# Position bias of a hybrid decoder step: tables laid out on the host in place of tables built on the chip and spread in DRAM

## The chip, the cores and the metric

The kernel runs on one core of one Trainium2 chip. The metric is the device time of one execution in microseconds; the runs of the kernel before have a median of 2324.24 us. The engines are TensorE (PE for its matmuls, PEld for its weight loads), VectorE (DVE), ScalarE (ACT), GpSimd (POOL) and SyncE (SP). Transfers run on 16 DMA engines. SP's transfers travel on queue q1 ("hardware dynamic" in the profile), POOL's on queue q0 ("software dynamic").

## What is computed

One step of a two-layer decoder on 320 tokens, 256 of a prompt and 64 of eight sample sequences of eight tokens. A layer projects x (2048 channels) to 13824 columns, runs three branches on them and merges these:

```python
h = x @ w_in
oa, s_new = retention(qa, ka, va, s_ret, pos0)
p = multi_scale_pool(u_ext, pos0, T)
oc = window_attention(qc, k_ext, v_ext, pos0, sinks, rel_bias)
merged = sigmoid(ma) * ya + sigmoid(mb) * yb + sigmoid(mc) * yc
x_new = layer_norm(alpha * x + merged @ w_out, ln_g, ln_b)
```

The change touches the window attention. It has 16 heads in 4 key groups, a window of 128 and a bias on the scores that depends on head and distance alone (32 buckets of distances; beyond the window a score is masked):

```python
dist = arange(bq)[:, None] + WINDOW - arange(span)[None, :]
bias = rel_bias[t5_bucket(maximum(dist, 0))]
s = where(valid, s + bias, finfo(float32).min)
```

The sample sequences also attend to 128 cached keys and values each (`cache_win_k`, `cache_win_v`).

## The kernel before, in words

All weights are cut on the host into 128 x 128 blocks in the order of use, eight blocks to a chunk of 512 KB. `load` (line 148) fetches a chunk from SP's queue, `split_h` (ACT, the copy of line 177) and `split_l` (mostly DVE, line 184) split it into a high and a low part, and a block takes three matmuls of 128 x 128 by 320 columns (line 198). A chunk is 24 such matmuls. In `run`, while TensorE works on chunk c, ACT and DVE split chunk c + 2, and SP is given the load of chunk c + 6. Four tiles `w` hold raw chunks, three `h` and three `l` hold split ones, so a load waits until the split of an older chunk has freed a tile.

After each chunk `pump` lets background work emit a step: `setup`, the attention, the retention and the pooling are generators. This fixes each engine's own order of instructions, but not the time: an engine runs ahead until it meets a wait. `setup` gives POOL almost nothing but transfers.

The order at the start: SP loads x and the first chunks in turns; x is split too (`xh` by ACT, `xl` by DVE). The first product group takes eight chunks, along with x as it comes.

The bias before: `setup` loads the 32 buckets of 16 heads to `rb` (line 323), memsets `zt` [16, 384], fills it by one ACT copy and 16 small DVE copies (line 331), then POOL writes `zt` 128 times into a DRAM tile `zd` [16, 128, 384] (line 336, 3 MB). Behind it on POOL stand the loads of the constants: `dmask`, `qdec`, `maskS`, `kdec`, `kdecS`, `cnt`, `pscale`, `lng`, `lnb`, `bmask`, `flip` (line 138). Reading `zd` with a row step of 383 gives each query's row a shift by one. So `load_bias` in `attention` (line 825) reads [128, 4, 256] in rows of 1 KB on SP, twice for each of two head pairs and layers, and the table of the samples, `biasS` [128, 4, 160], is memset and filled by 32 small transfers on SP (line 361). The cached values `cv` come from a natural layout in rows of 512 B (`done_kc`, line 763), the cached keys `ck` by partition.

Of the kernel before, what the change touches and what calls it, by code (L numbers as in the profile page):

```python
# [11 lines left out]
F32 = mybir.dt.float32  # L12
# [6 lines left out]
DEPTH = 2  # L19
NP = 256                 # prompt tokens, columns 0..255  # L20
NB, NT = 8, 8            # sample sequences and their tokens, columns 256 + 8 b + t
# [3 lines left out]
POOL_BUF = 15  # L25
POOL_W = (2, 4, 8, 16)
EXT = POOL_BUF + NP      # prompt part of a pooling row, then NB parts of HW
# [4 lines left out]
ROW = 128 * 384  # L32
# [6 lines left out]
CH = 8                   # weight blocks of 128 x 128 in a chunk  # L39


def att_rows(t):
    """Columns of tile t = 4 P + g of the attention: head (2P, g), then head (2P + 1, g)."""
    p, g = divmod(t, 4)
    lo, hi = (2 * p) * 4 + g, (2 * p + 1) * 4 + g
    return np.concatenate([np.arange(lo * 64, lo * 64 + 64), np.arange(hi * 64, hi * 64 + 64)])
# [6 lines left out]
def layer_groups():  # L53
    """Products of a layer in their order; the jobs of one group share their K loop."""
    g = [[("kc", 0), ("vc", 0), ("qc", 0), ("qc", 1)]]
    g += [[("qc", t)] for t in (2, 3)]
    g += [[("kc", 1)], [("vc", 1)]] + [[("qc", t)] for t in (4, 5, 6, 7)]
    late = [("ub", i) for i in range(8)]
    for h in range(HA):
        late += [("qa", h), ("ka", h), ("va", 2 * h), ("va", 2 * h + 1)]  # L60
    for i, job in enumerate(late):
        g.append([job])
        if i in (4, 6, 8, 10):
            g += [[("pm", i - 4)], [("pm", i - 3)]]
    for b in "bac":
        g += [[("g" + b, i)] for i in range(8)]
        for j in range(0, 16, 2):
            g += [[("m" + b, j)], [("m" + b, j + 1)], [("y" + b, j)], [("y" + b, j + 1)]]
    g += [[("wo", j)] for j in range(16)]
    return g  # L70


def layer_blocks():
    """(kind, index, k) of each 128 x 128 block of weights, in the order of use."""
    out = []
    for grp in layer_groups():
        for k in range(n_k(grp[0][0])):
            out += [(kind, i, k) for kind, i in grp]
    return out
# [7 lines left out]
def free(ap):  # L87
    """Elements of a partition."""
    return math.prod(ap.shape[1:])
# [9 lines left out]
class Step:  # L99
    def __init__(self, ctx, tc, io):  # L100
        self.tc, self.nc, self.io = tc, tc.nc, io
        pool = lambda n, b, **kw: ctx.enter_context(tc.tile_pool(name=n, bufs=b, **kw))
        self.cp = pool("const", 1)
        self.gp = pool("gran", 24)
        self.mp = pool("mid", 13)
        self.np = pool("mini", 6)
        self.sp = pool("small", 8)
        self.wp = pool("w", 4)
        self.hp = pool("wh", 3)
        self.lp = pool("wl", 3)  # L110
        self.pd = pool("psd", 3, space=bass.MemoryType.PSUM)
        self.pp = pool("psp", 5, space=bass.MemoryType.PSUM)
        self.dp = pool("dram", 1, space=bass.MemoryType.DRAM)
        self.raw, self.H, self.L = {}, {}, {}
        self.busy = {"a": 0.0, "v": 0.0, "p": 0.0}
        self.lanes = {"att": deque(), "ret0": deque(), "ret1": deque()}
        self.misc = []

# [81 lines left out]
    def add_mm(self, out, lhsT, rhs):  # L200
        """Adds to a part of what an earlier matmul of the bank wrote."""
        self.nc.tensor.matmul(out, lhsT=lhsT, rhs=rhs, start=False, stop=True, skip_group_check=True)  # L202
# [6 lines left out]
    def hl(self, h, lo, src):  # L209
        """The two parts of src whose sum it is."""  # L210
        self.copy(h, src)
        self.tt(lo, src, h.bitcast(F32), ALU.subtract)

    def rsqrt(self, y, v, t):
        """y = v ** -0.5 of t = v ** 0.5, with one step of Newton's."""
        self.busy["v"] += 0.8
        self.nc.vector.reciprocal(out=y, in_=t)
        self.stt(t, y, -0.5, y, ALU.mult, ALU.mult)
        self.tt(t, t, v, ALU.mult)
        self.stt(y, t, 1.5, y, ALU.add, ALU.mult)  # L220

    def sums(self, out, src, first):
        """Sums over the partitions, of the tokens 80 g + i at partitions 32 g.. and column i."""
        for g in range(4):
            o = out[32 * g:32 * g + 32, :]
            a = src[:, 80 * g:80 * g + 80]
            if first:
                self.mm(o, self.ones[:, 0:32], a)
            else:
                self.add_mm(o, self.ones[:, 0:32], a)  # L230

    def fold(self, y):
        """For spread(): of a group's 32 equal rows one with the high part of y, the next the low one."""
# [8 lines left out]
    def spread(self, r):  # L242
        """The inverse of the order of sums(): a row of all tokens at each partition."""
        ps = self.p([128, T])
        self.mm(ps, self.ones_r, r.rearrange("p g i -> p (g i)"))
        return ps

    def token_sums(self, src):
        """Sums over the partitions, with tokens 0.., 128.. and 192.. at the partitions of a column."""
# [5 lines left out]
    def token_rows(self, y):  # L255
        """The inverse of token_sums() for y: a row of all tokens at each partition."""
# [26 lines left out]
    def pump(self):  # L283
        """Once a chunk: background steps, as far as the other engines keep up with TensorE."""
# [16 lines left out]
    def setup(self):  # L301
# [19 lines left out]
        zt = self.m([16, 384], name="zt")  # L321
        rb = self.m([16, 32], name="rb")
        nc.sync.dma_start(out=rb, in_=io["rel"])
        nc.vector.memset(zt, NEG)
        yield
        yield
        self.copy(zt[:, 240:256], rb[:, 16:32])
        for n in range(16, 32):
            a = BUCKET_START[n]
            b = (BUCKET_START + [128])[n + 1] - 1  # L330
            nc.vector.tensor_copy(
                out=zt[:, 255 - b:256 - a],
                in_=rb[:, 31 - n:32 - n].to_broadcast([16, b - a + 1]),
            )
        zd = self.dp.tile([16, 128, 384], F32, name="zd")
        nc.gpsimd.dma_start(out=zd, in_=zt.unsqueeze(1).to_broadcast([16, 128, 384]))
        self.zd = zd[:]
        yield
# [12 lines left out]
        self.biasS = self.const("biasS", [128, 4, 160])  # L351
        nc.vector.memset(self.biasS, NEG)
        for _ in range(8):
            yield
        for kv in range(4):
            row = self.zd.offset + 4 * kv * ROW
            for b4 in range(4):
                r = slice(32 * b4, 32 * b4 + 32)
                for o, n, c0 in ((127, 128, 0), (255, 8, 128 + 8 * b4)):
                    src = bass.AP(self.zd.tensor, row + o, [[ROW, 4], [383, 8], [1, n]])  # L360
                    nc.sync.dma_start(out=self.biasS[r, kv, c0:c0 + n], in_=src)
                if b4 % 2:
                    yield

# [72 lines left out]
    def block_low(self, jobs, k):  # L437
        """The products with the low parts of the activations; the end of the jobs."""
# [55 lines left out]
    def before(self, kind, i):  # L494
# [4 lines left out]
        if kind == "mb" and i == 0:  # L499
            for o, src in (("o_wkc", "ckr"), ("o_wvc", "cv")):  # L500
# [254 lines left out]
    def done_kc(self, p, ps):  # L755
# [7 lines left out]
        nc.sync.dma_start(  # L763
            out=cv, in_=self.io["cv"][l, :, :, 128 * p:128 * p + 128].rearrange("b s d -> s b d")
        )
# [15 lines left out]
    def softmax(self, s, n, sink, nsink):  # L781
        """s: n score tiles [128, keys] in a row, normalised in place, in three stages."""
# [22 lines left out]
    def attention(self, l, p, a):  # L805
# [15 lines left out]
        def load_bias(hf):  # L821
            b = self.g([128, 4, 256], name="bias")
            row = 4 * (2 * p + hf) * ROW
            src = bass.AP(self.zd.tensor, self.zd.offset + row + 127, [[383, 128], [ROW, 4], [1, 256]])
            nc.sync.dma_start(out=b, in_=src)
# [19 lines left out]
        # second block's scores: rows of q's two parts against k's high part, then q's high part and k's low one  # L845
# [15 lines left out]
        def soft(make, out):  # L861
            """The stages of one softmax: scores, softmax (3), what comes of it."""
# [12 lines left out]
        def block0(hf):  # L875
            """The first 128 queries: their own keys."""
# [27 lines left out]
        def block1(hf, g):  # L904
            """The other queries: all keys of both blocks."""
# [34 lines left out]
        def sample(c):  # L940
            """Four sequences: rows 32 b + 8 g + t, the cached keys and the new ones of the four."""
# [268 lines left out]

def weight_blocks(a):
# [89 lines left out]
```

## Time and profile before

| | |
|---|---|
| median of 3 runs | 2324.24 us (2323.37 to 2325.18) |
| profiled execution, span | 2325.7 us |
| PE busy | 2275.5 us (98%) |
| DVE, ACT, POOL busy | 1221.6, 946.1, 183.8 us |
| chain that ended last | PE 91%, DVE 5%, DMA 2%, ACT 1% |
| DMA, mean over the span | 154 GB/s |

How to read it: the page cuts the span into 40 slices of 58 us and gives each engine's busy share in tenths, then the clock that TensorE was granted, then the DMA engines' busy share. The groups name line, engine, operation and tiles as out<-in. The lists of waits name who waited for whom. A timeline row has start, duration, engine, line, operation, tiles, shape and count, and in brackets the idle time of that engine just before and what ended it. A row of a stretch table has the stretch, its length, then busy time and instruction count of PE, PEld, DVE, ACT and POOL, then the granted clock as a share of 2.4 GHz, the DMA engines' busy share and GB/s.

### The profile page before, as it was taken

To read this page: it belongs to the slowest core of one execution; us is meant where nothing else is said; L and a number is where in the kernel's file an instruction comes from. 1 tells how busy PE (TensorE), PEld (TensorE's weight loads), DVE (VectorE), ACT (ScalarE), POOL (GpSimd) and SP (SyncE) were. 2 spreads that over 40 slices of the span, in tenths; PEclk is the share of its full clock that TensorE was granted. 3 is DMA by queue.
4 is the path that set the end of the run, shared out by engine and by line. 5 is a ranking of instruction groups with operands and counts; after the bars stand their busy time and mean duration, and the time that the engine had idled before them with its cause. 6 is when DMAs were issued, how large, how long until landed. Compare 5 with 4: busy or idle time off the path is not lost.

```text
span 2325.7 us, 37758 instructions
## 1 busy us (share of the span) xinstructions
PE 2275.5 (98%) x15660; PEld 2219.8 (95%) x15660; DVE 1221.6 (53%) x1844; ACT 946.1 (41%) x1537; POOL 183.8 (8%) x190
## 2 busy tenths in 40 slices
PE   8799999999999999999999999999999999999997
PEld 8697999999999999999998989999999999999997
DVE  4459555443444444446666785554344444444566
ACT  4354444433333334333355444453334333433333
POOL 0114100000000000000041140000000000000001
PEclk9899999999999999999999999999999999999998
DMA  8743545444444444444444334544444444444442
GB/s 224 215 140 107 171 154 198 167 145 154 145 154 145 154 147 153 145 155 145 150 162 138 138 128 157 192 175 154 153 146 146 153 154 145 146 154 147 153 146 99
DMA packets 106091, 358.00 MB, mean 154 GB/s; under 512 B 12192, under 2 KB 21344, under 8 KB 105856
## 3 DMA queue, kind: packets, MB, share of 16 engines
q1 hardware_dynamic: 101152, 336.15, 42.1%
q0 software_dynamic: 4768, 19.45, 3.1%
q8 instruction: 122, 2.00, 0.3%
q14 instruction: 49, 0.40, 0.1%
HBM read 338.46 MB, written 21.03 MB: 155 GB/s over the span
## 4 chain that ended last, share of the span: by engine, by line
PE 91%; DVE 5%; DMA 2%; ACT 1%; issue 0%; SPq 0%; DVEq 0%; ACTq 0%
PE d L198 85%; PE p L198 4%; DMA w<-w 2%; DVE win L184 1%; PE p L207 1%; PE p L202 1%; DVE l L184 1%; DVE sc L193 0%; DVE s L188 0%; DVE z L184 0%; DVE s L184 0%; DVE s L786 0%; DVE pp L188 0%; DVE sc L188 0%; DVE pp L184 0%
## 5 line engine op out<-in xcount | busy, mean ns | idle before, releaser
L198 PE MATMUL d<-xh,h 128*128 128x320 f32 x3424 | 1073.9, 314 | 28.9 <-ACT h L177 13.6
L184 DVE TENSOR_TENSOR l<-w,h 128x1024 fp32r<-128x1024 f32 (+1 forms) x562 | 699.2, 1245 | 745.4 <-ACT h L177 745.0
L198 PE MATMUL d<-xh,l 128*128 128x320 f32 x3424 | 1061.1, 310 | 2.0 <-DVE l L184 2.0
L198 PE MATMUL d<-xl,h 128*128 128x320 f32 x3424 | 1050.3, 310 | 0.0
L177 ACT ACTIVATE h<-w 128x1024 fp32r<-128x1024 f32 (+1 forms) x597 | 627.6, 1052 | 518.5 <-PE d L198 363.4
L198 PEld LDWEIGHTS d<-xh,h 128*128 128x128 f32 x3424 | 646.2, 189 | 42.3 <-ACT h L177 14.2
L198 PEld LDWEIGHTS d<-xh,l 128*128 128x128 f32 x3424 | 646.4, 189 | 3.3 <-DVE l L184 2.8
L198 PEld LDWEIGHTS d<-xl,h 128*128 128x128 f32 x3424 | 642.9, 189 | 0.0
L198 PE MATMUL d<-mgh,h 128*128 128x320 f32 x512 | 158.7, 310 | 0.0
L198 PE MATMUL d<-mgh,l 128*128 128x320 f32 x512 | 158.2, 309 | 0.0
L198 PE MATMUL d<-mgl,h 128*128 128x320 f32 x512 | 158.2, 309 | 0.0
L177 ACT ACTIVATE sig<-d 128x320 f32<-128x320 f32 x96 | 42.0, 438 | 225.5 <-PE d L198 225.5
L184 POOL TENSOR_TENSOR l<-w,h 128x1024 fp32r<-128x1024 f32 x35 | 85.3, 2443 | 226.5 <-ACT h L177 198.8
L198 PEld LDWEIGHTS d<-mgh,l 128*128 128x128 f32 x512 | 96.1, 188 | 0.2
L198 PEld LDWEIGHTS d<-mgh,h 128*128 128x128 f32 x512 | 96.1, 188 | 0.2
L198 PEld LDWEIGHTS d<-mgl,h 128*128 128x128 f32 x512 | 96.1, 188 | 0.0
L184 POOL TENSOR_TENSOR acc<-acc,ya 128x320 f32<-128x320 f32 x32 | 28.2, 881 | 822.2 <-DVE ya L184 822.2
L198 PE MATMUL d<-gbh,h 128*128 128x320 f32 x256 | 79.1, 309 | 0.0
L198 PE MATMUL d<-gbh,l 128*128 128x320 f32 x256 | 79.1, 309 | 0.0
L198 PE MATMUL d<-gbl,h 128*128 128x320 f32 x256 | 79.1, 309 | 0.0
L198 PE MATMUL d<-gah,h 128*128 128x320 f32 x256 | 79.1, 309 | 0.0
L198 PE MATMUL d<-gah,l 128*128 128x320 f32 x256 | 79.1, 309 | 0.0
(238 smaller groups left out, 2118.4 us busy)
## 6 DMA issues: line engine op xcount, KB each, us to landing
w<-w SPq DMA_DIRECT2D x595, 512.0 KB
s<-s SPq DMA_DIRECT2D x16, 512.0 KB
o_rets<-s POOLq DMA_DIRECT2D x16, 512.0 KB, 5.3
bias<-zd SPq DMA_DIRECT2D x8, 512.0 KB
zd<-zt POOLq DMA_DIRECT2D x1, 3072.0 KB, 35.4
o_x<-z SPq DMA_DIRECT2D x8, 320.0 KB
ck<-ck SPq DMA_DIRECT2D x4, 512.0 KB
cv<-cv SPq DMA_DIRECT2D x4, 512.0 KB
```

What stands on the lines that cost most here:

```text
L177: self.nc.scalar.activation(out=out, in_=in_, func=func, **kw)
L184: (eng or self.nc.vector).tensor_tensor(out=out, in0=a, in1=b, op=op)
L198: self.nc.tensor.matmul(out, lhsT=lhsT, rhs=rhs, start=start, stop=stop)
L202: self.nc.tensor.matmul(out, lhsT=lhsT, rhs=rhs, start=False, stop=True, skip_group_check=True)
L207: self.nc.tensor.transpose(out, in_, ident[:n, :n])
```

## The change

The host makes two tables from `rel_bias`: `bias_p` [4, 128, 4, 256], for each key group, query and head a row over 256 keys, and `bias_s` [128, 4, 160], the sample table. `rb`, `zt` and `zd` are gone, with their copies, the 3 MB write and the DRAM tile. `biasS` is now one POOL transfer of 320 KB after the constants, without memset, and `load_bias` reads 4 KB from each partition's place. The cached values are handed in twice: `cvr` as before, for the copy from DRAM to DRAM into the output, and `cv` by partition, read in rows of 4 KB. The products, their order and the other operations are the same.

```diff
@@ setup
-        zt = self.m([16, 384], name="zt")
-        rb = self.m([16, 32], name="rb")
-        nc.sync.dma_start(out=rb, in_=io["rel"])
-        nc.vector.memset(zt, NEG)
-        yield
-        yield
-        self.copy(zt[:, 240:256], rb[:, 16:32])
-        for n in range(16, 32):
...
-        zd = self.dp.tile([16, 128, 384], F32, name="zd")
-        nc.gpsimd.dma_start(out=zd, in_=zt.unsqueeze(1).to_broadcast([16, 128, 384]))
-        self.zd = zd[:]
-        yield
         self.dmask = self.const("dmask", [128, HA, 128], io["c_dmask"])
...
         self.flip = self.const("flip", [128, 2], io["c_flip"])
         yield
-        self.biasS = self.const("biasS", [128, 4, 160])
-        nc.vector.memset(self.biasS, NEG)
-        for _ in range(8):
-            yield
-        for kv in range(4):
...
-                    nc.sync.dma_start(out=self.biasS[r, kv, c0:c0 + n], in_=src)
+        self.biasS = self.const("biasS", [128, 4, 160], io["bias_s"])
@@ before
-            for o, src in (("o_wkc", "ckr"), ("o_wvc", "cv")):
+            for o, src in (("o_wkc", "ckr"), ("o_wvc", "cvr")):
@@ done_kc
-        nc.sync.dma_start(
-            out=cv, in_=self.io["cv"][l, :, :, 128 * p:128 * p + 128].rearrange("b s d -> s b d")
-        )
+        nc.sync.dma_start(out=cv, in_=self.io["cv"][l, p])
@@ load_bias
-            row = 4 * (2 * p + hf) * ROW
-            src = bass.AP(self.zd.tensor, self.zd.offset + row + 127, [[383, 128], [ROW, 4], [1, 256]])
-            nc.sync.dma_start(out=b, in_=src)
+            nc.sync.dma_start(out=b, in_=self.io["bias_p"][2 * p + hf])
@@ host
+def bias_tables(rel):
...
+    return dict(bias_p=bp.transpose(2, 0, 3, 1), bias_s=bs.transpose(0, 2, 1))
-        cv=a["cache_win_v"].reshape(DEPTH, NB, 128, 256),
+        cv=a["cache_win_v"].reshape(DEPTH, NB, 128, 2, 128).transpose(0, 3, 2, 1, 4),
+        cvr=a["cache_win_v"].reshape(DEPTH, NB, 128, 256),
-        rel=a["rel_bias"].T[:, ::-1],
+        **bias_tables(a["rel_bias"]),
```

## Rows read from the trace of the kernel before

**Rows 1.** The page: busy us, share, instructions; DMA tenths in 40 slices.

```profile
PE 2275.5 (98%) x15660; PEld 2219.8 (95%) x15660; DVE 1221.6 (53%) x1844; ACT 946.1 (41%) x1537; POOL 183.8 (8%) x190
...
DMA  8743545444444444444444334544444444444442
```

**Rows 2.** PE's waits, whole span: us in total, times, longest us.

```profile
PE d L198 <- ACT h L177: 13.6, 2, 12.6
PE d L198 <- DVE rt L184: 6.7, 2, 3.3
```

**Rows 3.** Stretches of 5 us around the long wait (columns as told above).

```profile
50.00:55.00 5.00, 5.00 (x36) 5.00 (x35) 0.00 (x0) 0.00 (x0) 0.00 (x0) 1.00 1.02 169
...
65.00:70.00 5.00, 0.00 (x0) 0.00 (x0) 0.00 (x0) 0.00 (x0) 1.61 (x3) 0.50 1.03 274
```

**Rows 4.** Chain that ended last, in time: start us, us, what, count.

```profile
32.79 40.32 DMA w<-w x2
...
126.40 3.52 PE d L198 x24
```

**Rows 5.** Timeline of ACT, the split whose chunk came late.

```profile
73.20 1.06 ACT L177 ACTIVATE h<-w 128x1024 fp32r<-128x1024 f32 x1 [16.11 <-DMA w<-w]
```

**Rows 6.** DMA queues, 36 to 60 us: packets, MB, share of 16 engines.

```profile
q0 software_dynamic: 493, 2.27, 83.5%
q1 hardware_dynamic: 417, 1.55, 15.8%
```

**Rows 7.** Timelines of POOL and DVE: POOL's last computation at the start, zt, zd.

```profile
1.02 0.29 POOL masks.py:199 TENSOR_SCALAR_AFFINE_SELECT ident<-ident 128x128 f32<-128x128 f32 x1
...
29.92 1.24 DVE L331 COPY zt<-rb 16x3 f32<-16x3 f32 x16
...
31.87 1.24 POOL L336 DMA_DIRECT2D zd<-zt  x1 [30.56 <-DVE xl L184]
```

**Rows 8.** Timeline of PE around the long wait.

```profile
56.82 0.41 PE L198 MATMUL d<-xh,h 128*128 128x320 f32 x1 [1.02 <-ACT h L177]
58.08 0.41 PE L198 MATMUL d<-xh,l 128*128 128x320 f32 x1 [0.85 <-DVE l L184]
...
61.40 0.31 PE L198 MATMUL d<-xl,h 128*128 128x320 f32 x1
74.31 0.64 PE L198 MATMUL d<-xh,h 128*128 128x320 f32 x1 [12.60 <-ACT h L177]
...
81.60 0.31 PE L198 MATMUL d<-xl,h 128*128 128x320 f32 x1
```

**Rows 9.** Timeline of SP's queue: cached values in layer 1 and layer 2.

```profile
40.52 4.36 SPq L763 DMA_DIRECT2D cv<-cv  x1
...
1198.88 0.42 SPq L763 DMA_DIRECT2D cv<-cv  x1
```

**Rows 10.** Stretch of layer 2 that loads caches and bias.

```profile
1200.00:1240.00 40.00, 40.00 (x270) 38.80 (x269) 17.69 (x22) 17.41 (x29) 2.57 (x8) 1.00 0.68 230
```

**Rows 11.** DMA traffic, 8 to 20 us.

```profile
DMA packets 1178, 4.65 MB, mean 387 GB/s; under 512 B 134, under 2 KB 134, under 8 KB 1178
```

**Rows 12.** Timelines of ACT, DVE and PE: the split of chunk 2.

```profile
13.03 1.06 ACT L177 ACTIVATE h<-w 128x1024 fp32r<-128x1024 f32 x1 [1.09 <-DMA w<-w]
...
14.90 1.22 DVE L184 TENSOR_TENSOR l<-w,h 128x1024 fp32r<-128x1024 f32 x1
...
16.17 0.41 PE L198 MATMUL d<-xh,l 128*128 128x320 f32 x1
```

**Rows 13.** Stretches of the start.

```profile
3.00:5.00 2.00, 0.24 (x1) 0.24 (x1) 0.62 (x2) 0.99 (x2) 0.00 (x0) 1.00 0.76 204
5.00:8.00 3.00, 3.00 (x12) 2.92 (x12) 0.47 (x2) 0.44 (x1) 0.00 (x0) 1.00 0.87 302
```

**Rows 14.** Stretches with the 3.3 us waits for rt in layers 1 and 2.

```profile
215.00:225.00 10.00, 6.45 (x56) 5.43 (x55) 9.62 (x19) 4.36 (x14) 5.20 (x4) 1.00 0.45 160
...
1355.00:1365.00 10.00, 6.54 (x48) 5.34 (x47) 9.65 (x18) 4.34 (x15) 6.05 (x4) 0.83 0.38 142
```

More of the change, by code (lines that the diff above doesn't have):

```diff
@@ L31 @@
 NEG = -3.0e38
-ROW = 128 * 384
 ALPHA = (2.0 * DEPTH) ** 0.25
@@ L112, in __init__ @@
         self.pp = pool("psp", 5, space=bass.MemoryType.PSUM)
-        self.dp = pool("dram", 1, space=bass.MemoryType.DRAM)
         self.raw, self.H, self.L = {}, {}, {}
@@ L320, in setup @@
         self.ts(self.nsinkS, self.sinkS, -1.0)
-        zt = self.m([16, 384], name="zt")
-        rb = self.m([16, 32], name="rb")
-        nc.sync.dma_start(out=rb, in_=io["rel"])
-        nc.vector.memset(zt, NEG)
-        yield
-        yield
-        self.copy(zt[:, 240:256], rb[:, 16:32])
-        for n in range(16, 32):
[L329 to L333, printed above, removed]
-            )
-        zd = self.dp.tile([16, 128, 384], F32, name="zd")
-        nc.gpsimd.dma_start(out=zd, in_=zt.unsqueeze(1).to_broadcast([16, 128, 384]))
-        self.zd = zd[:]
-        yield
         self.dmask = self.const("dmask", [128, HA, 128], io["c_dmask"])
@@ L350, in setup @@
         yield
-        self.biasS = self.const("biasS", [128, 4, 160])
-        nc.vector.memset(self.biasS, NEG)
-        for _ in range(8):
-            yield
-        for kv in range(4):
[L356 to L360, printed above, removed]
-                    nc.sync.dma_start(out=self.biasS[r, kv, c0:c0 + n], in_=src)
-                if b4 % 2:
-                    yield
+        self.biasS = self.const("biasS", [128, 4, 160], io["bias_s"])
     def run(self):
@@ L762, in done_kc @@
         cv = self.g([128, NB, 128], name="cv")
-        nc.sync.dma_start(
-            out=cv, in_=self.io["cv"][l, :, :, 128 * p:128 * p + 128].rearrange("b s d -> s b d")
-        )
+        nc.sync.dma_start(out=cv, in_=self.io["cv"][l, p])
         self.att[p] = dict(kv=kv, ck=ck, cv=cv)
@@ L1208, in constants, with table @@
     return {k: np.ascontiguousarray(v, dtype=f) for k, v in c.items()}
+def bias_tables(rel):
+    bucket = np.searchsorted(np.array(BUCKET_START), np.arange(128), side="right") - 1
+    row = np.concatenate([rel[bucket], np.full((1, 16), NEG, np.float32)])
+    def table(dist):
+        return row[np.where((dist >= 0) & (dist < 128), dist, 128)]
+    q, k = np.arange(128), np.arange(256)
+    bp = table(128 + q[:, None] - k[None, :]).reshape(128, 256, 4, 4)
+    b4, g, t = np.arange(128) // 32, np.arange(128) % 32 // 8, np.arange(128) % 8
+    c = np.arange(160)
+    new = t[:, None] - (c[None, :] - 128) % 8
+    own = (c[None, :] - 128) // 8 == b4[:, None]
+    dist = np.where(c[None, :] < 128, 128 + t[:, None] - c[None, :], np.where(own, new, -1))
+    bs = table(dist).reshape(128, 160, 4, 4)[np.arange(128), :, :, g]
+    return dict(bias_p=bp.transpose(2, 0, 3, 1), bias_s=bs.transpose(0, 2, 1))
 def weight_blocks(a):
```

## The prediction

> **What bounds the kernel now.** I read the page's busy times first: PE is busy for 98% of the span, so nothing done on DVE, ACT, SP or POOL is worth anything unless PE waits for it [rows 1]. The next view is therefore PE's list of waits. Its longest entry is a wait of 12.6 us for the high part `h` of a weight chunk [rows 2]. The page's DMA line says where to look: most slices stand at 3 to 5 tenths, the first two at 8 and 7 [rows 1]. The table of stretches then shows the place. Up to 55 us PE is full; from 65 to 70 us it does nothing at all, while the DMA engines are fully busy, and the granted clock is down to 0.50, that is 1.2 GHz [rows 3]. The chain of waits has one piece of 40.32 us there, a weight load that lands late [rows 4]; ACT idled 16.11 us for it [rows 5].
>
> What keeps the DMA engines busy is seen by queue. Between 36 and 60 us q0 has 83.5% of the time of all 16 engines for 493 packets, and q1, which carries the weights, 15.8% for 417 [rows 6]. So a packet of q0 took 0.835 x 16 x 24 / 493 = 0.65 us for 4.6 KB, one of q1 0.158 x 16 x 24 / 417 = 0.145 us for 3.7 KB. The two queues take turns about packet by packet, so q1 is held to 1.55 MB in 24 us, 65 GB/s, where PE uses a chunk of 524 KB every 3.52 us [rows 4], 149 GB/s. The loads ahead last until about 56 us, then PE starves. POOL's transfer in that time is the write of `zd`, issued at 31.87 us [rows 7].
>
> The Trainium skill, page "SBUF — State Buffer", section "Door 1: The DMA port swizzle", says that a transfer's bandwidth depends on how many of the 16 memory ports its partitions reach. By its formula the 16 partitions of `zt` reach four, an estimate of about 109 GB/s; the row has q0 at 2.27 MB in 24 us, 95 GB/s, and the trace agrees. This only makes it likelier that a constant, which lies on 128 partitions, isn't slow on q0.
>
> **The change part by part.**
>
> *The write of `zd` goes.* What PE lost around it [rows 8]: it idled 1.02 us before the matmul at 56.82 us. The next step took 58.08 - 56.82 = 1.26 us where one takes 3.52 / 24 = 0.147 us [rows 4]: 1.11 us. From the matmul at 61.40 to that at 81.60 us lie 24 steps, 3.52 us at full clock; they took 20.20 us: 16.68 us, of which about 2.7 us is the half clock after the standstill. Together 18.8 us. Without `zd`, what is late next in this stretch? The remaining loads are `ck`, `cv` and `bias`. Layer 2 has the same loads with no write of `zd`, in the old row sizes: PE is busy 40.00 of 40.00 us there, at full clock [rows 10]. SP's issue of `cv` took 4.36 us in layer 1 and 0.42 us in layer 2 [rows 9], so its length belonged to the crowded queues. Hence all of the 18.8 us goes.
>
> *The constants move to the front.* POOL's queue is in order. Before, its first transfer was `zd`, which waited 30.56 us for `zt` [rows 7]; the constants stood behind that wait. Now nothing on POOL waits, so the constants are issued from 1.31 us on, the end of the row before, into the loading of x and the first weights. Their size: by their shapes `dmask`, `qdec` and `maskS` have 256 KB each, `bmask` 160 KB, the seven small ones 91 KB together; `biasS` adds 128 x 640 x 4 B = 320 KB: 1339 KB, or 1.37 MB. At the start the DMA engines move 387 GB/s [rows 11], so this is 3.54 us of all 16 engines. Who waits: PE runs at the pace of the arriving chunks. Chunk 2's high split waited for the load until 13.03 us, its low split ended at 14.90 + 1.22 = 16.12 us, and PE took it at 16.17 us [rows 12]; there is no slack. What can hide the new traffic is the idle share of the engines before: 0.24 x 2 + 0.13 x 3 = 0.87 us between 3 and 8 us [rows 13]. So PE starts later by 2.7 to 3.5 us if all constants come before chunk 2, and by some 2.2 us if `biasS`, the last issue, comes behind it. I take 3.0 us. Bounds: 0, if q0 gets in only where q1 leaves room, and 12.0 us, if q0 is as slow as for `zd`: 1.37 MB at 95 GB/s is 14.4 us, in which q1 still moves 65 / 387 of its own, 2.4 us [rows 6, 11].
>
> The Trainium skill, page "DMA: Bandwidth & Descriptors", section "Where 436 GB/s comes from", puts a core's limit from HBM at about 358 GB/s; the row has 387 GB/s over 12 us, so the measurement decides. By the page the constants would cost 3.8 us and the sum 0.3 us more.
>
> *Edits at nothing.* The 16 copies and two memsets of `zt` and `biasS` on DVE, the ACT copy, the load of `rb`, the 32 fills of `biasS` on SP: none is on a path to which PE listens, since PE has full stretches around them (50 to 55 us, for one) and DVE is 53% busy [rows 1, 3]. Bound: DVE's 16 copies at 29.92 us take 1.24 us ahead of a low split [rows 7]; if PE listened to that split they would be worth those 1.24 us. Larger rows for `bias` and `cv` shorten transfers that already lie beside full PE work [rows 10]: nothing, in either direction. Background work is emitted as before; the pace counter of ACT loses one copy of 0.2 us, in a stretch in which it stands at its floor.
>
> *The sum.* 18.8 - 3.0 = 15.8 us. Of the profiled span 2325.7 us that leaves 2309.9; the median of the runs is 1.5 us below that span, so 2324.2 - 15.8 = 2308.4 us.
>
> **The rivals.**
>
> (a) *The start hides the constants.* Then only the stall counts: 2324.2 - 18.8 = 2305.4 us. For it: 0.87 us is free before 8 us, and later chunks have some slack. Against: chunk 2 has none [rows 12].
>
> (b) *q0 is slow whatever it carries.* The start then loses 12.0 us: 2324.2 - 18.8 + 12.0 = 2317.4 us. For it: no row shows q0 at speed beside a full q1 for long. Against: the constants come to 128 partitions, not from 16.
>
> (c) *The clock falls once more.* Two waits of 3.3 us for `rt` are alike in both layers; in layer 1 the clock held (1.00), in layer 2 it fell (a mean of 0.83 over 10 us is 3.4 us at 1.2 GHz, so 1.7 us lost, and it may last beyond the stretch) [rows 2, 14]. With everything shifted, layer 1's may fall, or the later start may run on 1.2 GHz for longer. The standstill's half clock cost 2.7 us; one or two such events give 2308.4 + 2 to 5 = 2310 to 2313 us. It can also go the other way, layer 2's fall vanishing: 2308.4 - 1.7 or twice that, 2305 to 2307.
>
> (d) *The stall stays, and the start is later: slower.* If it was not `zd` that held the weights up but the loads of `ck` and `cv`, 512 KB each, behind which they queue on q1 (`cv` held SP for 4.36 us just before [rows 9]), removing `zd` frees nothing, and the constants still cost 3.0 us: 2324.2 + 3.0 = 2327.2 us. It decides if q1's own packets ahead of the late chunk, and not q0's share, set its landing. Against: q1 had only 15.8% of the engines [rows 6], and layer 2 does without a stall [rows 10].
>
> **How the numbers follow.** Forecast 0.55, (a) 0.20, (b) 0.11, (c) 0.09, (d) 0.05. The likeliest case gives 2308.4 us. The range runs from 2302.5 (case (a) with layer 2's fall of the clock gone as well) to 2317 us; it leaves out (d) and the far half of (b). About 0.2%, 4.65 us, is what a measurement can tell from no change: faster means under 2319.6, which holds all cases but (d) and a little of (b): 0.93. Case (d) lies within 0.2% for the most part: same 0.05, slower 0.02.
>
> **What the changed profile would show.** Right: no wait of PE for `h` over 1 us between 30 and 90 us, and a granted clock of 1.00 through that stretch; q0 gone from it but for small stores; POOL's first constant issued near 1.3 us; the low split of chunk 2 ending near 19 us in place of 16.1 and PE's steady run beginning that much later; layer 2 of the same length. Wrong: a wait for `h` that stays at 56 to 75 us (d); the first steady chunk later by over 6 us (b); chunk 2's low split still at 16.1 us (a); other stretches at clock 0.50 than before (c). The prediction fails altogether if the constants are issued late after all, or if some wait of PE after 90 us grows, since the sum takes all of that as unchanged.

## The result and the profile after

| | before | after |
|---|---|---|
| median of the timed runs, first comparison | 2324.6 us (4 runs) | 2311.5 us (2309.0 to 2312.5, 4 runs) |
| ratio, 95% interval | | 0.9939 [0.9927, 0.9951] |
| second comparison (below) | 2325.6 us (8 runs) | 2308.7 us (2307.5 to 2311.2, 5 runs) |
| ratio, 95% interval | | 0.9929 [0.9916, 0.9942] |
| profiled execution, span | 2325.7 us | 2309.0 us |

The change is faster by 13.1 us in the first comparison and by 16.9 us in the second; the profiled pair differs by 16.7 us. The forecast was 15.8 us.

The page after, its busy times and DMA tenths, answers [rows 1]:

```profile
PE 2273.1 (98%) x15660; PEld 2218.0 (96%) x15660; DVE 1222.3 (53%) x1826; ACT 945.8 (41%) x1536; POOL 182.9 (8%) x190
...
DMA  7433455444444444444353344554444444444442
```

PE is busy 2.4 us less, though it does the same 15660 matmuls: that is mostly the half clock after the standstill. The second DMA slice fell from 7 to 4 tenths. PE's list of waits, against [rows 2]:

```profile
PE d L196 <- ACT xh L175: 6.9, 3, 5.0
PE d L196 <- DVE rt L182: 6.7, 2, 3.3
```

The wait for `h` is gone altogether; `rt` is as it was. The stretches of [rows 3, 13], after:

```profile
3.00:5.00 2.00, 0.00 (x0) 0.00 (x0) 0.69 (x1) 1.10 (x2) 2.00 (x5) 1.00 0.87 240
5.00:8.00 3.00, 2.97 (x11) 2.97 (x12) 0.49 (x1) 0.00 (x0) 1.50 (x3) 1.00 0.99 339
...
50.00:55.00 5.00, 5.00 (x36) 5.00 (x35) 1.23 (x1) 1.97 (x3) 0.24 (x1) 1.00 0.55 161
65.00:70.00 5.00, 5.00 (x36) 4.69 (x35) 4.55 (x6) 3.16 (x5) 0.54 (x1) 1.00 0.81 261
```

PE is full from 65 to 70 us, at full clock. The DMA engines have gone from fully busy to 0.55 between 50 and 55 us, and they are busier in the first 8 us. The queues from 36 to 60 us, against [rows 6], show why:

```profile
q1 hardware_dynamic: 1554, 5.68, 70.0%
q0 software_dynamic: 96, 0.20, 2.1%
```

q1 moves 5.68 MB in place of 1.55 MB. The timelines of POOL, DVE and PE at the start, against [rows 7, 12]:

```profile
1.47 0.77 POOL L136 DMA_DIRECT2D dmask<-c_dmask  x1 [0.16 <-issue]
...
10.45 0.53 POOL L136 DMA_DIRECT2D flip<-c_flip  x1 [1.86 <-DMA maskS<-c_masks]
10.98 0.54 POOL L136 DMA_DIRECT2D biasS<-bias_s  x1
...
16.80 1.22 DVE L182 TENSOR_TENSOR l<-w,h 128x1024 fp32r<-128x1024 f32 x1
...
18.08 0.41 PE L196 MATMUL d<-xh,l 128*128 128x320 f32 x1 [0.61 <-DVE l L182]
...
22.14 0.31 PE L196 MATMUL d<-xh,h 128*128 128x320 f32 x1
...
64.74 0.31 PE L196 MATMUL d<-xl,h 128*128 128x320 f32 x1
```

The constants are issued from 1.47 us on, and chunk 2's low split ends at 16.80 + 1.22 = 18.02 us, 1.9 us later than before. Both traces hold the same 15660 matmuls in the same order, so they can be matched one by one. The matmul at 22.14 us stood at 19.93 us before, in this row of the trace before: 2.2 us later.

```profile
19.93 0.31 PE L198 MATMUL d<-xh,h 128*128 128x320 f32 x1
```

That at 64.74 us is the one that stood at 81.60 us [rows 8]: 16.9 us earlier. Between them 2.2 + 16.9 = 19.1 us were won, and from there to the end the shift moves by no more than 0.15 us. The second pair of profiled executions, from the experiments below, gives 2.6 us later at the start and 18.8 us won.

### The profile page after: what moved, and what is told of

Its sections match the earlier page's. It is cut to its first block, busy times and chain, and to the rows that moved or that the text cites. A ratio compares the mean times of both kernels' runs of the same rounds, so it can differ in the third digit from the quotient of the medians.

```text
span 2309.0 us, 37695 instructions
## 1 busy us (share of the span) xinstructions
PE 2273.1 (98%) x15660; PEld 2218.0 (96%) x15660; DVE 1222.3 (53%) x1826; ACT 945.8 (41%) x1536; POOL 182.9 (8%) x190
## 4 chain that ended last, share of the span: by engine, by line
PE 93%; DVE 5%; ACT 0%; DMA 0%; issue 0%; SPq 0%; DVEq 0%
PE d L196 87%; PE p L196 4%; DVE win L182 1%; PE p L205 1%; PE p L200 1%; DMA w<-w 0%; DVE sc L191 0%; DVE l L182 0%; DVE s L186 0%; DVE z L182 0%; DVE s L182 0%; DVE s L752 0%; DVE pp L186 0%; DVE sc L186 0%; DVE pp L182 0%
## 5 line engine op out<-in xcount | busy, mean ns | idle before, releaser
L196 PE MATMUL d<-gch,l 128*128 128x320 f32 x256 | 79.2, 309 | 0.0
L196 PE MATMUL d<-gal,h 128*128 128x320 f32 x256 | 79.2, 309 | 0.0
L196 PE MATMUL d<-gcl,h 128*128 128x320 f32 x256 | 79.2, 309 | 0.0
```

Of the source, the lines that this page charges most:

```text
L196: self.nc.tensor.matmul(out, lhsT=lhsT, rhs=rhs, start=start, stop=stop)
```

## The experiments

**The kernel before once more,** unchanged, to learn how times, spans and the profiled execution stand to each other.

> The kernel before, unchanged, for its spread. The profiled pair says 2325.7 - 2309.0 = 16.7 us, the timed medians 13.1 us. Theory A: an execution is timed about 1.7 us above its span, as in the runs of the changed kernel, and the profiled execution of before was a slow one; then the spans here lie at 2321.5 to 2323.5 us, and the stall in them is some 3 us shorter than the 18.8 us read. Theory B: the spans lie at 2325 to 2326 us again, the time is below the span for this kernel, and the stall is the same.

Eleven runs gave a median of 2325.15 us (2323.5 to 2327.1). In every run the time lies 1.7 to 1.8 us above the span, as for the changed kernel; the spans of nine lie at 2321.7 to 2323.8 us, one at 2325.4 us and that of the profiled run at 2325.2 us. So theory A holds on the offset: by it the profiled execution of before, with a span of 2325.7 us, took some 2327.4 us and was 2.8 us slower than the median. That its stall was longer by as much isn't shown: the timed runs leave no trace, and the second profiled execution had nearly the same stall (12.4 us in its longest wait).

**Constants later,** behind the first store of keys on POOL.

```diff
+        for _ in range(6):
+            yield
         self.dmask = self.const("dmask", [128, HA, 128], io["c_dmask"])
```

> The changed kernel, with six more steps of set-up ahead of the constants, so that on POOL they stand behind the store of the first keys, which waits until about 40 us. Theory (constants at the start delay the first chunks): the low split of chunk 2 ends at 16.1 us again, and the time is 2.2 us below the changed kernel, 2309.3 us against 2311.5. Rival (the start is later for another reason): same as the changed kernel, 2311.5 us. Second rival (the constants, 1.37 MB, now crowd the chunks at 40 to 50 us): a wait of PE for h there and more than 2311.5 us.

It took 2307.6 us (2305.5 to 2309.4), ratio to before 0.9925 [0.9912, 0.9937]; 2309.3 us had been expected. Timelines of POOL, DVE and PE, and two stretches, of this run:

```profile
38.49 0.55 POOL L136 DMA_DIRECT2D dmask<-c_dmask  x1
...
14.31 1.22 DVE L182 TENSOR_TENSOR l<-w,h 128x1024 fp32r<-128x1024 f32 x1
...
15.59 0.42 PE L196 MATMUL d<-xh,l 128*128 128x320 f32 x1
...
200.00:210.00 10.00, 9.51 (x61) 8.58 (x62) 9.62 (x28) 6.61 (x20) 4.06 (x3) 0.67 0.35 134
35.00:60.00 25.00, 24.91 (x171) 24.62 (x170) 8.16 (x7) 10.06 (x17) 10.14 (x19) 1.00 0.82 283
```

With the constants issued at 38.5 us, chunk 2's low split ends at 15.5 us, earlier than the 16.1 us expected, and PE takes it 2.5 us earlier than in the changed kernel, 2.8 us from chunk 3 on. The constants were what delayed the start. Between 35 and 60 us PE is busy for 24.91 of 25 us, so they cost nothing there. The trace also shows rival (c) of the prediction: after the 3.3 us wait for `rt` in layer 1, ending near 200.5 us, the granted clock fell (mean 0.67 over ten us). Matched matmuls fall 2.0 us further back there against the changed kernel, and get 0.9 us of it back at 211 us, where the changed kernel waits for `sc` and this run doesn't: 1.1 us in all. A wait of 0.4 us for `sc` at 122 us, which the changed kernel hasn't, takes some more, so the two profiled spans differ by 1.4 us only (2309.0 and 2307.6 us).

**Old row sizes:** the changed kernel with the bias read in rows of 1 KB and the cached values in rows of 512 B.

```diff
-        nc.sync.dma_start(out=cv, in_=self.io["cv"][l, p])
+        nc.sync.dma_start(
+            out=cv, in_=self.io["cvr"][l, :, :, 128 * p:128 * p + 128].rearrange("b s d -> s b d")
+        )
-            nc.sync.dma_start(out=b, in_=self.io["bias_p"][2 * p + hf])
+            nc.sync.dma_start(out=b, in_=self.io["bias_p"][2 * p + hf].rearrange("g q k -> q g k"))
```

The host lays the bias table out accordingly.

> The changed kernel, with the bias tables read in rows of 1 KB and the cached values in rows of 512 B, as before; the write in DRAM stays away. Theory (row sizes are hidden beside full PE work): 2311.5 us, within 1.5 us. Rival (the smaller packets were part of what held the weights up): a wait for h between 40 and 75 us and some 3 to 15 us more, 2315 to 2326 us.

It took 2310.0 us (2309.3 to 2311.1), 1.6 us below the changed kernel's first median, inside its spread, and 1.2 us above its second (below). Two stretches of this run:

```profile
14.00:17.00 3.00, 3.00 (x12) 3.00 (x12) 1.24 (x4) 1.78 (x3) 0.00 (x0) 0.50 1.01 398
...
40.00:80.00 40.00, 39.91 (x268) 38.70 (x268) 17.70 (x22) 17.45 (x33) 3.04 (x8) 1.00 0.68 233
```

PE is full where the small rows are read: the new layouts of `cv` and `bias` are worth nothing measurable. At the start this execution had clock 0.50 from 14 to 17 us; by matched matmuls it left the start 0.4 us later than the profiled one of the changed kernel, and from there to the end the shift stays at 0.3 to 0.5 us.

**The same 3 MB from 128 partitions,** in the kernel before. It leaves out that the heads differ; all read head 0's bias.

```diff
-        zt = self.m([16, 384], name="zt")
+        zt = self.m([128, 384], name="zt")
...
-        nc.gpsimd.dma_start(out=zd, in_=zt.unsqueeze(1).to_broadcast([16, 128, 384]))
+        nc.gpsimd.dma_start(out=zd.rearrange("h q c -> q h c"), in_=zt.unsqueeze(1).to_broadcast([128, 16, 384]))
```

> The kernel before, with the same 3 MB written to the DRAM tile in the same rows of 1.5 KB, but from 128 partitions in place of 16. It leaves out that heads differ: all get head 0's bias. Theory A (the write was slow because its source lies on 16 partitions): packets of the write take 0.07 to 0.2 us, the write is over in 10 to 15 us and the stall is gone: 2324.6 - 18.8 = 2306 us, or 2309 if the stall was shorter in the timed runs. Theory B (writes of this size to DRAM are slow from anywhere): the packets stay at about 0.65 us for 4.6 KB and the time at 2324.6 us.

It took 2307.8 us (2305.7 to 2308.0), ratio 0.9924 [0.9910, 0.9937]. The queues from 36 to 45 us, in which q0 carries little but the write; the write from issue to landing, in this run and before; and the stretch from 40 to 60 us:

```profile
q0 software_dynamic: 567, 2.61, 78.6%
q1 hardware_dynamic: 217, 0.83, 22.6%
...
zd<-zt POOLq DMA_DIRECT2D x1, 3072.0 KB, 16.7
zd<-zt POOLq DMA_DIRECT2D x1, 3072.0 KB, 35.4
...
40.00:60.00 20.00, 20.00 (x139) 19.97 (x138) 6.12 (x5) 8.06 (x13) 4.52 (x11) 1.00 1.05 372
```

A packet of q0 took 0.786 x 16 x 9 / 567 = 0.20 us for 4.6 KB, where it took 0.65 us for 4.6 KB [rows 6], and PE has no stall. While the write runs, q1 still gets only 0.83 MB in 9 us, 92 GB/s, less than the 149 GB/s that PE uses; but the write has landed 16.7 us after its issue, a little more than the 10 to 15 us expected, at 48 us and so before the loads ahead are used up. The bytes, the row size, the queue and the DRAM target are those of before: spreading the source over the partitions took the stall away.

**The right tables from 128 partitions:** the kernel before with each head on eight partitions, so that nothing is left out.

```diff
-        zt = self.m([16, 384], name="zt")
-        rb = self.m([16, 32], name="rb")
-        nc.sync.dma_start(out=rb, in_=io["rel"])
+        zt = self.m([128, 384], name="zt")
+        rb = self.m([128, 32], name="rb")
+        nc.sync.dma_start(out=rb, in_=io["rel"].unsqueeze(1).to_broadcast([16, 8, 32]))
...
-        nc.gpsimd.dma_start(out=zd, in_=zt.unsqueeze(1).to_broadcast([16, 128, 384]))
+        nc.gpsimd.dma_start(out=zd.rearrange("h (j r) c -> (h j) r c", j=8), in_=zt.unsqueeze(1).to_broadcast([128, 16, 384]))
```

> The kernel before with its tables built on the chip and spread in DRAM, as they are, but each head's row lies on eight partitions, 128 in all, and each of these is written 16 times in place of 128 times from 16 partitions. Theory (the source's 16 partitions made the write slow): packets of the write near 0.19 us for 4.6 KB as in the run with one head's bias, no stall, constants behind the write and out of the start: 2307.8 us. Rival (that run was quick only because all heads read the same 1.5 KB): packets above 0.4 us and a stall of 5 to 19 us, 2313 to 2325 us.

It took 2306.5 us (2305.5 to 2307.9), ratio 0.9919 [0.9905, 0.9933]. Queue q0 from 36 to 45 us, then the stretch in which before stood still:

```profile
q0 software_dynamic: 502, 2.31, 68.1%
...
60.00:80.00 20.00, 20.00 (x132) 18.83 (x131) 11.54 (x18) 10.95 (x29) 0.93 (x2) 1.00 0.65 222
```

A packet of 4.6 KB took 0.681 x 16 x 9 / 502 = 0.20 us, and there is no stall. In the run above each partition's rows went to places far apart in DRAM; here, as before, they are neighbours, so the order of the rows isn't what made the difference. With more partitions each one is also read fewer times, 16 in place of 128; these runs don't part the two. Tables built on the chip and spread in DRAM are no slower here than tables from the host, once the spreading starts from all partitions, with the constants behind it and out of the start. This version and the changed kernel with later constants (below) have the lowest medians of all.

**The changed kernel, and the one with later constants, side by side.**

> The changed kernel, unchanged, beside the others on one chip. Theory: 16.6 us below the kernel before where the traces are compared (18.8 us of stall less 2.2 us at the start), and 13 to 15 us by the timed medians, 2310 to 2312 us.

> The changed kernel with the constants behind the store of the first keys, beside the changed kernel itself. Theory: 2.2 us (the later start by the trace) to 2.8 us below it, less up to 1.8 us if the clock falls after the wait for rt in layer 1 as it did in the first such run: 1 to 3.9 us below. Rival (the gap of 3.9 us between the first two medians was the difference of two sessions): no gap.

The changed kernel took 2308.7 us (2307.5 to 2311.2), ratio 0.9929 [0.9916, 0.9942], below the 2310 to 2312 us expected. With later constants it took 2306.9 us (2304.8 to 2308.9), ratio 0.9918 [0.9904, 0.9932]. The gap is 1.8 us, within the 1 to 3.9 us expected but with overlapping spreads; by matched matmuls of the two profiled executions it is 2.2 us, from chunk 3 on. In the later one's trace the clock held where it fell in the run above:

```profile
200.00:210.00 10.00, 8.53 (x69) 7.48 (x70) 9.65 (x28) 6.93 (x22) 3.96 (x3) 1.00 0.36 136
```

The same program, two executions, clock 0.67 and 1.00; the version with the right tables from 128 partitions had 0.83 over the same ten us. The timed runs spread with it: with later constants, the runs of this comparison that had a mean granted clock of 0.994 took 2304.8 and 2306.2 us, those with 0.991 and 0.992 2306.9 to 2308.9 us.

## Why the prediction was right, and where it was off

**The stall goes: right.** The step said 18.8 us, with the row sizes, `ck` and `cv` innocent. Matched matmuls give 19.1 us between chunk 3 and the stall's end, 18.8 us in the second pair. The runs with the write spread over 128 partitions show that the write alone was the cause, and the run with old rows that nothing else of the change helped. Rival (d) falls.

**Why the write was slow** was left in a sentence beside the sum; the runs now show its size: 0.65 us for a packet of 4.6 KB from 16 partitions, 0.20 us from 128. The Trainium skill, page "SBUF — State Buffer", section "Door 1: The DMA port swizzle", says that what counts is how many of the 16 ports a transfer's partitions reach; the trace agrees, in direction and in size (95 GB/s on q0 [rows 6], against an estimate of 109 GB/s for four ports).

**The constants at the start: right mechanism, 0.2 to 0.8 us too dear.** The step took 3.0 us of a possible 2.2 to 3.5; the trace has 2.2 us, the lower end, and for the reason given there: `biasS` came last, issued at 10.98 us. "Now nothing on POOL waits" was wrong: POOL waited for the landing of earlier constants ahead of `lnb`, `bmask` and `flip`, which spread the traffic out. Queue q0 after, from 4 to 12 us, and from 14.9 us, when the split of chunk 2 could start, to 18 us:

```profile
q0 software_dynamic: 425, 0.86, 33.0%
...
q0 software_dynamic: 81, 0.33, 27.1%
```

The 0.33 MB that came behind chunk 2 are the size of `biasS`. A packet of q0 took 0.33 x 16 x 8 / 425 = 0.10 us for 2.0 KB on average from 4 to 12 us, so rival (b) falls; rival (a) falls with the 1.9 us at chunk 2. Other pairs of executions give the cost as 2.6 us (the second pair), 2.8 us (the run with later constants) and 2.2 us (its repeat); the four executions with the constants behind `zd` left the start up to 0.7 us apart.

**The clock: a rival that does occur.** Rival (c) had 0.09 as a case of its own. It isn't a property of the change: layer 1's fall came in one of two executions of the same program. It belongs in the width of the range, with 1 to 2 us. The range's low end doesn't come out of its terms either: case (a) less layer 2's fall is 2305.4 - 1.7 = 2303.7 us, or 2302.0 us with twice that, not 2302.5.

**The base of the sum was wrong.** The step set the median 1.5 us below the profiled span and took that as an offset. The time of an execution is 1.7 us above its own span, and the profiled execution of before was 2.8 us slower than the median run. By spans the forecast was 2325.7 - 15.8 = 2309.9 us, and the profiled execution after had 2309.0. By medians the two comparisons gave 13.1 and 16.9 us; the first is short of the traces by 3.6 us, within its interval of 11 to 17 us. The runs go with the clock on both sides. In the first comparison two runs after had a mean granted clock of 0.990 and took 2312.3 and 2312.5 us, the other two 0.992 and 0.993, with 2310.7 and 2309.0 us. Of fifteen runs of before, beside the first experiments, three had 0.991 and took 2322.6 to 2324.7 us; the rest had 0.989 or 0.990 and took 2324.7 to 2328.5 us. Both profiled executions of before had 0.989. Where the clock fell in the timed runs isn't shown, and so it stays open whether a typical run of before has a shorter stall than the profiled ones.

**At nothing: right.** The DVE copies, the 32 fills and the row sizes moved nothing that can be seen: after the stall's end the shift stays the same to the end.

## What to carry to other kernels

A transfer that started from few partitions was dear here for everyone else on the DMA engines: look for a queue with a large share of their time and few bytes, and spread its source over all partitions before taking the work away. When a change removes the wait at the head of an in-order queue, list what stood behind it: it is now issued at once, here into the one stretch that had little spare DMA time, and a few empty steps were enough to place it better. Compare times with times and spans with spans, and take more than one profiled execution: the start and the clock differ between executions of one program.

## What had not been expected of the hardware

The factor: with the same bytes, row size, queue and target, a packet of the write took 0.65 us from 16 partitions and 0.20 us from 128, and while the slow one ran, q1, whose own packets took 0.145 us, fell to 65 GB/s. And that the clock's fall after a wait of 3.3 us differs between two executions of one program: 1.00 or 0.67 over the ten us behind it.
